# A transformer layer on one core: forget sums of the first FoX pair loaded earlier into another pool, late modulation begun earlier, and one ordering edge dropped in FoX

## The chip, the core and the metric

The kernel runs on one core of a Trainium2 chip. The metric is the time of one execution in microseconds (us). Before the change three runs took 3103.55 us in the median (3102.78 to 3106.61). TensorE (PE) multiplies matrices and transposes, and PEld is its weight load, shown apart. VectorE (DVE), ScalarE (ACT) and GpSimd (POOL) work elementwise. SyncE (SP) issues nearly all DMA transfers, one after the other in a fixed order: a transfer whose buffer is not free yet holds everything behind it in that queue.

## The reference

One decoder layer over 2048 tokens of width 1024, in float32:

```
mod = silu(c) @ w_ada + b_ada                  # six vectors: shift, scale, gate, twice
h = rms_norm(x, g_attn) * (1 + scale_a) + shift_a
q_f, k_f, v_f, q_s, k_s, v_s, f_logit = split(h @ w_in)
log_f = log_sigmoid(f_logit + b_fgate);  F = cumsum(log_f)
FoX, 8 heads:            softmax over s <= t of (q.k / 8 + F[t] - F[s]), times v
stick-breaking, 8 heads: A[t,s] = sigmoid(z_ts) * prod over s < j < t of (1 - sigmoid(z_tj)), times v
mix = concat(head_rms_norm(o_fox), head_rms_norm(o_sb))
x = x + gate_a * (mix @ w_out)
x = x + gate_m * (conv_ffn(rms_norm(x, g_mlp) * (1 + scale_m) + shift_m))
out = rms_norm(x, g_final)
```

F is the running sum of the log forget gates, one number per head and token; the text calls it the forget sums.

## The kernel before

Attention runs in 32 units: first 16 of stick-breaking, then 16 of FoX, each kind as four pairs of heads (p = 0 to 3) of four blocks of 512 tokens (tb = 0 to 3). A unit works through its two 256-query halves and its two heads. It forms logits on TensorE (lines 442 and 443, two matmuls of hi and lo parts), turns them into weights on DVE, ACT and POOL, transposes the weights on TensorE (L452), splits them into a high and a low part (ACT L456, DVE L457) and multiplies them with the values (L461). Later units of a pair have more keys and take longer.

Beside the attention run fillers. The projection of later units (`proj`, L284 for queries and keys, L355 for values) loads the modulated input `hs` in eight tiles of 512 KB (L410) into the ten buffers `hp`. `pace` says how many steps of it are due at each step of the attention, and `follow` draws them. From unit START = 3 on, the matmuls that a draw adds are tied behind the logits LAG = 12 entries back by `tc.issue_after`. That edge sets only an order on TensorE, no wait.

A second filler is the late modulation, `late_mod` (`lm`). It loads the convolution weights with 16 small DMAs (L593, L595) and transposes them. Then it goes through four of the six parts of `w_ada`: for each it loads eight 512 KB tiles (L607), scales them on ACT (L613) and sums them on POOL (L611, L614). Behind the first part comes `fold_out`: eight tiles of `w_out` are loaded (L577), scaled on DVE (L580), split on ACT and POOL and stored again (L584). All of this uses buffers of the same ten `hp`. It starts at unit LATE = 17, the second of FoX, with PER = 4 steps a unit.

In FoX a head needs its forget sums on all 128 partitions: tiles `Fb`, [128, 512], loaded from DRAM by a broadcasting DMA (L781), eight for each pair (two heads, four blocks). For the last chunk of keys POOL makes a masked copy `Fd` (L507). DVE adds `Fb` or `Fd` to the logits and keeps the row minimum `mn` (L509); ACT takes the exponential (L513).

Pools set the places. `px` holds the tiles of x for the first projection (tag `xt`, four buffers of [128, 1024]; later also the value tiles of stick-breaking pair 2) and small ones (tags `hf_a` and `z`). `sx` holds the intermediate tiles of stick-breaking. At the first FoX unit `sx` and `px` are closed and a pool `fx` is opened in their place, with ten buffers `Fb`, two `Fd`, one `sq` and others. A tile placed there has to wait for the last users of the old tiles at its place.

The order on each engine and in each queue comes from a scheduler that plays the program through when it is built: an instruction written later may be moved ahead of an earlier one that is not ready in that play.

Of the kernel before, what the change touches and what calls it, by code (L numbers as in the profile page):

```python
# [33 lines left out]
def kernel(ctx: ExitStack, tc: tile.TileContext, x, c, w_ada, b_ada, g_attn, w_in, b_fgate,  # L34
# [119 lines left out]
    def close_pool(*names):  # L154
        for name in names:
            pools.pop(name).close()
# [307 lines left out]
    def sb_head(j, qc, hl, Q, K, V, o):  # L464
        n = (2 * j + 2 + 3) // 4
        right = [None, None]
        for ch in range(n - 1, -1, -1):
# [18 lines left out]
            for m in range(0, nk, 2):  # L486
# [2 lines left out]
                         ch == n - 1 and m == 0, ch == 0 and m == nk - 2, kts[0] == 2 * j)  # L489
                yield  # L490

    def fox_head(j, qc, hl, Q, K, V, o, Fb, ls):
        n = (2 * j + 2 + 3) // 4
        rows_ = []
        for qi in range(2):
            W = (2 * j + qi + 1) * P
            a = sx.tile([P, S], F32, name="p", bufs=4)
            mn = None
            for ch in range(n):
                need = min(512, W - ch * 512)  # L500
                b = logits(max(need, 2 * P), slice((qc + qi) * P, (qc + qi + 1) * P), hl, Q, K[ch])
                sl = slice(ch * 512, ch * 512 + need)
                m2 = sx.tile([P, 1], F32, name="mn", bufs=8)
                add = Fb[ch]
                if ch == n - 1:
                    add = sx.tile([P, TB], F32, name="Fd", bufs=2)
                    nc.gpsimd.affine_select(out=add[:, :need], in_=Fb[ch][:, :need], pattern=[[-1, need]],  # L507
                                            base=need - P, channel_multiplier=1, compare_op=ALU.is_ge, fill=BIG)
                nc.vector.tensor_tensor_reduce(out=a[:, sl], in0=b[:, :need], in1=add[:, :need], scale=1.0,  # L509
                                               scalar=3e38 if mn is None else mn, op0=ALU.add, op1=ALU.min,  # L510
                                               accum_out=m2)
                mn = m2
            nc.scalar.activation(a[:, 0:W], a[:, 0:W], AF.Exp, scale=-1.0, bias=mn, accum_out=ls[:, hl, qc + qi:qc + qi + 1])  # L513
            rows_.append(a)
            yield
        for m in range(0, 2 * j + 2, 2):
            weighted(o, [m, m + 1], lambda kt, qi: rows_[qi][:, kt * P:(kt + 1) * P], V, hl, m == 0, m == 2 * j,
                     m == 2 * j)
            yield
# [10 lines left out]
    def attend(kind, p, tb, res, Fbs):  # L530
# [6 lines left out]
        mp = p if kind == "fox" else p + 4  # L537

        def head_var(j2):
            sq = sx.tile([P, 2 * P], F32, name="sq", bufs=1)  # L540
            cols_ = slice(j2 * 2 * P, (j2 + 1) * 2 * P)
            nc.gpsimd.tensor_mul(sq, oT[:, cols_], oT[:, cols_])

# [145 lines left out]
            yield max(first + (due - first) * min(1.0, m / (0.8 * n)),  # L689
                      base + (total - base) * (done + weight(units[i]) * m / n) / span if i >= START else 0)  # L690

    LAG = 12
    LATE, PER = 17, 4
    START, STOP = 3, 30

    HT = 2 * P
# [71 lines left out]
    for i, u in enumerate(units):  # L768
        kind, p, tb = u
        nxt = units[i + 1] if i + 1 < len(units) else None  # L770
        if u == ("sb", 1, 0):
            forget_sums()
        if u == ("fox", 0, 0):
            tick(1 << 20)
            close_pool("sx", "px")
            sx = open_pool("fx", side="right")
        if kind == "fox" and tb == 0:
            Fbs = [[sx.tile([P, TB], F32, name="Fb", bufs=10) for _ in range(NTB)] for _ in range(2)]
            for t in range(NTB):
                for h in range(2):  # L780
                    nc.sync.dma_start(Fbs[h][t],  # L781
                                      fs[2 * p + h:2 * p + h + 1, t * TB:(t + 1) * TB].to_broadcast([P, TB]))
        n = attend_steps(u)
        if i >= len(units) - 2:
            head_scale(i - len(units) + 2, pt(), sx)
# [9 lines left out]

        def follow(m):
            while projected[0] < goals[min(m, n - 1)]:
                with tc.issue_after(marks[max(0, len(marks) - 1 - LAG)]) if i >= START else nullcontext():
                    if next(ahead, 1) is not None:
                        break  # L800
            if nxt and projected[1] > i + 1 and loaded_units[0] == i + 1:
# [8 lines left out]
    tick(1 << 20)  # L810
    for t in range(2, NTB):
        head_scale(t, bank(psc, "bc", 2), p2a)
    close_pool("fx", "sb", "psb")

    psd = open_pool("psd", space=PSUM)
    ho = open_pool("hop0", side="right")
# [321 lines left out]
```

## Time and profile before

| | us |
|---|---|
| median of three runs | 3103.55 |
| the profiled execution, its own time | 3108.77 |
| its span, first to last instruction | 3106.8 |
| stick-breaking, to the store of its last unit | 0 to 884 |
| FoX, to about its last logits | 885 to 1540 |
| output projection | about 1540 to 1715 |
| up-projection and convolution | about 1715 to 2650 |
| down-projection | about 2650 to 3107 |

TensorE is busy for 95% of the span. Where the engine is busy all the time, the stage is as long as its matmuls. Idle stretches of TensorE, and stretches in which its granted clock (PEclk) is under 1, are what a change of order can win or lose. A row of the windows view gives, for a stretch of time, the length, then the busy time of PE, PEld, DVE, ACT and POOL with the number of instructions, then the granted clock, the busy share of the DMA engines and GB/s. In the timeline a row has start, length, engine, line and operation, and in brackets the idle time before it and what ended it.

### The profile page before, as it was taken

To read this page: it belongs to the slowest core of one execution; us is meant where nothing else is said; L and a number is where in the kernel's file an instruction comes from. 1 tells how busy PE (TensorE), PEld (TensorE's weight loads), DVE (VectorE), ACT (ScalarE), POOL (GpSimd) and SP (SyncE) were. 2 spreads that over 40 slices of the span, in tenths; PEclk is the share of its full clock that TensorE was granted. 3 is DMA by queue.
4 is the path that set the end of the run, shared out by engine and by line. 5 is a ranking of instruction groups with operands and counts; after the bars stand their busy time and mean duration, and the time that the engine had idled before them with its cause. 6 is when DMAs were issued, how large, how long until landed. Compare 5 with 4: busy or idle time off the path is not lost.

```text
span 3106.8 us, 45436 instructions
## 1 busy us (share of the span) xinstructions
PE 2957.1 (95%) x15934; PEld 2510.1 (81%) x15934; DVE 2063.9 (66%) x3206; ACT 1682.7 (54%) x3129; POOL 977.3 (31%) x1011
## 2 busy tenths in 40 slices
PE   6889999999989999999999899999999998999998
PEld 5788889889968888888877688888678887888887
DVE  6768778887856675667733677778977776254253
ACT  5657767777756665668634444444544443343332
POOL 1531322121122233333123344444444442332321
PEclk8999999999989999999999999999999999999999
DMA  9649756766387767775467522223222224565562
GB/s 270 228 133 318 217 186 204 265 222 215 123 265 235 223 217 271 241 266 162 167 197 228 189 76 82 83 87 89 85 82 82 82 82 145 184 203 166 183 203 86
DMA packets 312916, 546.79 MB, mean 176 GB/s; under 512 B 30992, under 2 KB 187408, under 8 KB 311664
## 3 DMA queue, kind: packets, MB, share of 16 engines
q1 hardware_dynamic: 301056, 531.27, 53.2%
q10 hardware_dynamic: 11632, 12.63, 1.2%
q8 instruction: 126, 2.06, 0.3%
q14 instruction: 102, 0.84, 0.1%
HBM read 407.14 MB, written 130.36 MB: 173 GB/s over the span
## 4 chain that ended last, share of the span: by engine, by line
PE 54%; DMA 15%; DVE 11%; POOL 7%; issue 7%; ACT 5%; SPq 1%; POOLq 0%; DVEq 0%; ACTq 0%
PE ps_pj L284 8%; PE ps_o L1077 8%; PE ps_pv L461 7%; PE ps_pt L452 6%; PE ps_pj L355 5%; PE ps_t L1077 4%; PE ps_bc L1077 4%; PE ps_qk L442 3%; PE ps_o L927 3%; PE ps_qk L443 3%; DMA wuraw<-in_w_up_dram 3%; DVE wu L45 3%; DMA hp<-in_w_ada_dram 2%; DVE u L996 2%; PE ps_o L736 2%
## 5 line engine op out<-in xcount | busy, mean ns | idle before, releaser
L927 PE MATMUL ps_o<-oa,wu 128*128 128x512 f32 x2088 | 505.6, 393 | 11.3 <-DVE oa L45 5.6
L927 PEld LDWEIGHTS ps_o<-oa,wu 128*128 128x128 f32 x2088 | 391.5, 189 | 103.2 <-DVE oa L45 9.3
L284 PE MATMUL ps_pj<-hp,w_qk 128*128 128x512 f32 x1512 | 417.0, 405 | 21.9 <-DMA hp<-hs 16.0
L457 DVE TENSOR_TENSOR at<-ps_pt,at 128x512 fp32r<-128x512 f32 (+1 forms) x576 | 364.9, 651 | 107.1 <-ACT at L456 104.5
L461 PE MATMUL ps_pv<-at,V 128*128 128x256 f32 x2304 | 408.2, 295 | 13.8 <-DVE at L457 5.6
L480 DVE TENSOR_TENSOR_SCAN a<-r,a 128x512 f32<-128x512 f32 (+2 forms) x320 | 363.1, 1153 | 82.8 <-POOL a L477 41.6
L456 ACT ACTIVATE at<-ps_pt 128x512 fp32r<-128x512 f32 (+1 forms) x576 | 319.3, 577 | 167.8 <-PE ps_pt L452 136.5
L461 PEld LDWEIGHTS ps_pv<-at,V 128*128 128x128 f32 x2304 | 336.7, 192 | 48.4 <-DVE at L457 14.6
L284 PEld LDWEIGHTS ps_pj<-hp,w_qk 128*128 128x128 f32 x1512 | 275.2, 191 | 79.0 <-DMA hp<-hs 20.8
L442 PE MATMUL ps_qk<-K,Q 128*128 128x512 f32 (+2 forms) x640 | 267.5, 419 | 20.4 <-DVE mn L509 11.7
L45 DVE TENSOR_TENSOR wd<-wdraw,wd 128x1024 fp32r<-128x1024 f32 x88 | 113.9, 1295 | 259.7 <-ACT wd L44 259.7
L1077 PE MATMUL ps_o<-wd,g 128*128 128x512 f32 x1040 | 250.1, 390 | 8.9 <-ACT g L44 8.9
L45 POOL TENSOR_TENSOR g<-graw,g 128x512 fp32r<-128x512 f32 x84 | 142.5, 1698 | 325.1 <-ACT g L44 317.9
L927 PE MATMUL ps_t<-ob,wu 128*128 128x512 f32 x984 | 241.8, 390 | 0.0
L443 PE MATMUL ps_qk<-K,Q 128*128 128x512 f32 (+2 forms) x640 | 238.7, 374 | 0.0
L1077 PEld LDWEIGHTS ps_o<-wd,g 128*128 128x128 f32 x1040 | 195.7, 188 | 50.0 <-ACT g L44 9.3
L355 PE MATMUL ps_pj<-w_v,hp 128*128 128x256 f32 (+1 forms) x1536 | 232.0, 289 | 3.6 <-DVE w_v L45 1.4
L44 ACT ACTIVATE wu<-wuraw 128x512 fp32r<-128x512 f32 x214 | 133.2, 626 | 188.4 <-PE ps_o L927 114.9
L355 PEld LDWEIGHTS ps_pj<-w_v,hp 128*128 128x128 f32 x1536 | 209.2, 191 | 13.6 <-DVE q L315 2.4
L927 PEld LDWEIGHTS ps_t<-ob,wu 128*128 128x128 f32 x984 | 185.3, 188 | 38.9 <-DVE y L979 0.2
L44 ACT ACTIVATE wd<-wdraw 128x1024 fp32r<-128x1024 f32 x88 | 93.0, 1057 | 207.0 <-PE ps_bc L1077 193.2
L474 ACT ACTIVATE r<-ps_qk 128x512 f32<-128x512 f32 (+2 forms) x320 | 172.9, 541 | 56.4 <-PE ps_qk L443 53.9
(222 smaller groups left out, 5490.1 us busy)
## 6 DMA issues: line engine op xcount, KB each, us to landing
hp<-hs SPq DMA_DIRECT2D x224, 512.0 KB
wuraw<-in_w_up_dram SPq DMA_DIRECT2D x84, 512.0 KB
wdraw<-in_w_down_dram SPq DMA_DIRECT2D x84, 512.0 KB
g<-u SPq DMA_DIRECT2D x42, 512.0 KB
graw<-g SPq DMA_DIRECT2D x84, 256.0 KB
hs<-hp SPq DMA_DIRECT2D x32, 512.0 KB
qk_fox<-q SPq DMA_DIRECT2D x32, 512.0 KB
Q<-qk_fox SPq DMA_DIRECT2D x64, 256.0 KB
```

The source lines that it names most:

```text
L44: nc.scalar.activation(hi, src, AF.Copy)
L45: (lo_engine or nc.gpsimd).tensor_sub(lo, src, f(hi))
L284: nc.tensor.matmul(acc, w[kt][:, a, n], h[:, bb], start=kt == 0 and i == 0, stop=kt == KT - 1 and i == 2)
L355: nc.tensor.matmul(av[:, t * width:(t + 1) * width], hts[kt][:, a, tok], w[1][kt][:, bb, 0:width], start=kt == 0 and m == 0, stop=kt == KT ...
L442: nc.tensor.matmul(b[:, :cw], Q[:, hl, 0, qcols], K[:, hl, :cw], start=True, stop=False)
L443: marks.append(nc.tensor.matmul(b[:, :cw], Q[:, hl, 1, qcols], K[:, hl, :cw], start=False, stop=True).ins)
L456: nc.scalar.activation(at[:, 0, lo:], b[:, lo:], AF.Copy)
L457: nc.vector.tensor_sub(at[:, 1, lo:], b[:, lo:], f(at[:, 0, lo:]))
L461: nc.tensor.matmul(o[:, 0:2 * P], V[kt // 4][:, kt % 4, hl, :], rhs, start=first and kk == 0 and w == 0, stop=last and kk == 1 and w == 1)
L480: nc.vector.tensor_tensor_scan(rev, r[:, 0:need][:, ::-1], rev, 0.0 if right[qi] is None else right[qi][:, 0:1], ALU.mult, ALU.add)
L927: nc.tensor.matmul(b, w[:, p, j], o[:, q], start=first and i == 0, stop=last and i == 2, skip_group_check=True)
L1077: nc.tensor.matmul(banks[t][n], g[:, a, t * P:(t + 1) * P], w[:, b, n * TB:(n + 1) * TB], start=k == 0 and i == 0, stop=k == NKD - 1 and i ...
```

## The change

There are four edits.

1. `Fb` becomes tiles of [128, 1024], each holding two blocks, in the four `xt` buffers of `px`, which now stays open through FoX: four loads of 512 KB a pair in place of eight of 256 KB. The first pair's loads are written at unit 14, two units ahead of FoX; those of the later pairs stay at the first unit of the pair. `Fd` and `sq` move into tags of `px` with two buffers each.
2. `late_mod` makes its first step (convolution weights) at unit 4 and the others from unit 12 on, the first unit of the last stick-breaking pair, three a unit in place of four.
3. `issue_after` is used for units 3 to 15 only, so not in FoX.
4. `px` is closed after FoX.

```diff
+    def load_sums(p):
+        sums = [[], []]
+        for t in range(0, NTB, 2):
+            for h in range(2):
+                b = px.tile([P, D], F32, name="Fb", tag="xt", bufs=4)
+                nc.sync.dma_start(b, fs[2 * p + h:2 * p + h + 1, t * TB:(t + 2) * TB].to_broadcast([P, D]))
+                sums[h] += [b[:, 0:TB], b[:, TB:D]]
+        return sums
...
-                    add = sx.tile([P, TB], F32, name="Fd", bufs=2)
+                    add = px.tile([P, TB], F32, name="Fd", tag="hf_a", bufs=2)
...
-            sq = sx.tile([P, 2 * P], F32, name="sq", bufs=1)
+            sq = (sx.tile([P, 2 * P], F32, name="sq", bufs=1) if kind == "sb" else
+                  px.tile([P, TB], F32, name="sq", tag="z", bufs=2)[:, 0:2 * P])
...
-    LAG = 12
-    LATE, PER = 17, 4
+    LAG, ENDQ = 12, 16
+    LATE, PER = 12, 3
...
         if u == ("sb", 1, 0):
             forget_sums()
+            next(lm)
         if u == ("fox", 0, 0):
             tick(1 << 20)
-            close_pool("sx", "px")
+            close_pool("sx")
             sx = open_pool("fx", side="right")
-        if kind == "fox" and tb == 0:
-            Fbs = [[sx.tile([P, TB], F32, name="Fb", bufs=10) for _ in range(NTB)] for _ in range(2)]
-            for t in range(NTB):
-                for h in range(2):
-                    nc.sync.dma_start(Fbs[h][t],
-                                      fs[2 * p + h:2 * p + h + 1, t * TB:(t + 1) * TB].to_broadcast([P, TB]))
+        if i == 14 or (kind == "fox" and tb == 0 and p):
+            Fbs = load_sums(p if kind == "fox" else 0)
...
-                with tc.issue_after(marks[max(0, len(marks) - 1 - LAG)]) if i >= START else nullcontext():
+                with tc.issue_after(marks[max(0, len(marks) - 1 - LAG)]) if START <= i < ENDQ else nullcontext():
...
-    close_pool("fx", "sb", "psb")
+    close_pool("fx", "px", "sb", "psb")
```

## The prediction, written before the changed kernel ran

> **What bounds the kernel now.** The page comes first: its span and the row of the granted clock, in 40 slices of 78 us.
>
> ```profile
> span 3106.8 us, 45436 instructions
> PEclk8999999999989999999999999999999999999999
> ```
>
> The slices say where to look, not why. The windows view over the stages that the change touches gives the lost time:
>
> ```profile
> 720.00:877.00 157.00, 155.93 (x1093) 143.92 (x1093) 126.24 (x170) 114.28 (x247) 19.85 (x36) 1.00 0.46 156
> 877.00:945.00 68.00, 54.98 (x274) 44.91 (x275) 30.49 (x88) 35.62 (x77) 24.16 (x33) 0.85 1.00 291
> 945.00:1540.00 595.00, 566.04 (x3710) 501.50 (x3709) 403.32 (x1033) 393.16 (x737) 180.29 (x243) 0.99 0.68 225
> 1540.00:1715.00 175.00, 158.53 (x746) 128.74 (x745) 65.56 (x120) 70.75 (x149) 47.45 (x57) 0.96 0.64 204
> ```
>
> In the last stick-breaking pair (720 to 877) TensorE idles 1.1 us of 157 at full clock: nothing is to be won there, only lost. At the passage into FoX (877 to 945) it idles 13.0 us of 68 and has a mean clock of 0.85, which is another 0.15 x 68 = 10.2 us: a hole of 23.2 us, with the DMA engines busy all the time (share 1.00). The rest of FoX idles 29.0 us of 595 and loses about 0.01 x 595 = 6 us of clock. I read the hole in steps of 4 us, then by its waits:
>
> ```profile
> 882.00:886.00 4.00, 1.14 (x6) 0.96 (x6) 0.16 (x1) 0.00 (x0) 0.00 (x0) 0.77 0.94 259
> 886.00:890.00 4.00, 2.69 (x7) 1.16 (x5) 0.00 (x0) 0.00 (x0) 0.00 (x0) 0.50 0.98 382
> 890.00:894.00 4.00, 4.00 (x12) 3.01 (x13) 1.27 (x7) 1.49 (x6) 1.45 (x5) 0.50 0.83 245
> ...
> 906.00:910.00 4.00, 1.76 (x4) 1.05 (x5) 2.38 (x7) 1.66 (x4) 2.84 (x5) 0.76 0.99 384
> 910.00:914.00 4.00, 4.00 (x28) 3.58 (x27) 3.53 (x12) 2.12 (x6) 0.99 (x3) 0.81 1.04 324
> 914.00:918.00 4.00, 2.33 (x13) 1.37 (x12) 3.03 (x11) 3.98 (x9) 4.00 (x5) 1.00 1.05 217
> 918.00:922.00 4.00, 3.67 (x12) 3.19 (x13) 0.65 (x3) 2.17 (x6) 2.34 (x3) 0.54 1.03 229
> 922.00:926.00 4.00, 4.00 (x21) 3.82 (x20) 1.23 (x4) 1.40 (x5) 0.00 (x0) 0.61 1.02 406
> ```
>
> The last column but two is the clock. It falls behind each hole in TensorE's work. Four microseconds at 0.50 cost 2.0 us, so the three losses are: 882 to 894, 0.92 + 2.0 + 2.0 = 4.9 us; 906 to 914, 0.96 + 0.76 = 1.7 us; 918 to 926, 1.84 + 1.56 = 3.4 us. Together that is 10.0 of the 10.2 us.
>
> The chain of work that ended last (start, length, what) goes through transfers here, so these microseconds count in full:
>
> ```profile
> 876.25 7.63 DMA V<-vs_fox
> ...
> 886.80 8.20 DMA Fb<-fs
> ...
> 906.68 11.60 DMA hp<-hs
> ```
>
> One of the three is of the sums; values and `hs` hold the others. The waits of TensorE in 877 to 945:
>
> ```profile
> PE ps_pj L284 <- DMA hp<-hs: 6.1, 4, 2.9
> PE ps_qk L442 <- DVE mn L509: 4.8, 1, 4.8
> ```
>
> And in 945 to 1540:
>
> ```profile
> PE ps_pj L284 <- DMA hp<-hs: 8.8, 8, 2.4
> PE ps_qk L442 <- DVE mn L509: 6.9, 10, 2.3
> PE ps_pv L461 <- ACT at L456: 4.6, 5, 2.0
> PE ps_pt L452 <- DVE at L457: 2.8, 1, 2.8
> ```
>
> The timeline shows what stands behind them:
>
> ```profile
> 877.48 0.60 PE L452 MATMUL ps_pt<-edge,a 128*128 128x128 f32 x4
> 877.84 1.32 PE L461 MATMUL ps_pv<-at,V 128*128 128x256 f32 x8
> 885.30 7.17 SPq L781 DMA_DIRECT2D Fb<-fs  x8
> 891.83 0.64 POOL L507 TENSOR_SCALAR_AFFINE_SELECT Fd<-Fb 128x128 f32<-128x128 f32 x2 [10.08 <-DMA Fb<-fs]
> 904.02 3.11 POOL L611 TENSOR_SCALAR hp<-hp,cs 128x512 f32<-128x512 f32 x2 [8.62 <-DMA hp<-in_w_ada_dram]
> 908.24 0.79 PE L442 MATMUL ps_qk<-K,Q 128*128 128x512 f32 x1 [4.76 <-DVE mn L509]
> ...
> 1086.53 1.41 DVE L580 SCALAR_TENSOR_TENSOR hp<-hp,cols 128x512 f32<-128x512 f32 x2 [3.38 <-DMA hp<-in_w_out_dram]
> 1088.60 0.81 PE L452 MATMUL ps_pt<-edge,p 128*128 128x128 f32 x4 [2.80 <-DVE at L457]
> 1102.63 0.69 PE L442 MATMUL ps_qk<-K,Q 128*128 128x384 f32 x1 [2.29 <-DVE mn L509]
> ```
>
> The sums are issued at 885.30, behind the last stick-breaking work, and POOL can mask only at 891.83. At 904.02 POOL has waited 8.62 us for a tile of the late modulation, with the next masks queued behind it; DVE, and then the logits at 908.24, wait for them. At 1086.53 the same happens on DVE: the fold of `w_out` waits 3.38 us for its DMA at the head of DVE's queue, and TensorE idles 2.80 us for a split that stands behind it.
>
> **The change, part by part.** The sum is made on the profiled execution, 3108.77 us (span 3106.8 and 2.0 around it); that is 5.2 us above the median of the runs, 3103.55, and I carry the difference over unchanged.
>
> *The passage.* In the order of the changed kernel the four loads stand behind the values of stick-breaking pair 2, some 300 us early, and the first masks are made before the passage. The late modulation's first tiles are summed before it too, so no L611 stands in front of a mask. The 4.8 us wait goes whole: -4.8. What is late next are the `hs` tiles. Half of them still stand in SP's queue behind the store of the last stick-breaking unit, but the eight sums (7.17 us of issue) and the 16 convolution DMAs no longer stand around them: I take half of the 6.1 us, -3.0. The thin end of the stick-breaking chain stays. Of the clock, the 1.7 us behind the wait that goes returns whole, and a third of the other two losses, (4.9 + 3.4) / 3 = 2.8: -4.5. Not more, because two of the chain's three transfers stay; but in the changed order the keys of the last block stand in SP's queue ahead of that store, no longer behind the sums. Together -12.3, between 0 (the transfers keep the hole open) and -23.2.
>
> By the Trainium skill's page "TensorE: Matmul & The Clock Gate" (Part 1: The HAM clock gate) the clock halves only after about one idle window of 3.4 us and returns after as long a busy one, so holes shorter than that would cost no clock. The half clock at 886 to 894 agrees with the lower of its two rates. By it the whole 10.2 us would return, in place of 4.5, and the sum would be lower by 5.7. The row 918 to 922 speaks against it: 0.54 behind a window with 1.67 us idle.
>
> *The fold of `w_out`* moves from about 1010 to 1190 into about 880 to 1010. It leaves the start of the second pair, where it and its clock cost this:
>
> ```profile
> 1088.00:1092.00 4.00, 3.40 (x15) 3.01 (x16) 4.00 (x12) 3.35 (x8) 2.97 (x3) 0.62 0.43 167
> 1092.00:1096.00 4.00, 4.00 (x19) 3.60 (x18) 3.94 (x11) 2.85 (x7) 1.25 (x2) 0.53 1.00 306
> ...
> 1100.00:1104.00 4.00, 1.71 (x9) 1.22 (x9) 3.51 (x8) 3.72 (x8) 1.96 (x3) 0.83 1.05 410
> 1104.00:1108.00 4.00, 4.00 (x26) 3.81 (x26) 3.69 (x10) 2.79 (x5) 1.76 (x3) 0.74 0.96 334
> ```
>
> That is 2.8 + 2.3 us of waits and 4 x (0.38 + 0.47 + 0.17 + 0.26) = 5.1 us of clock, 10.2 in all. But its loads now meet the stretch where the DMA engines have no share left, and a late one stands again at the head of DVE's queue, in front of L509. Bounds are -10.2 (nothing comes back) and +10.2 (twice as much does). I take +2: the same again and a little more, since the share is 1.00 there.
>
> *The rest of the late modulation in stick-breaking.* Until FoX there are 14 scalings on ACT, at this row:
>
> ```profile
> L613 ACT ACTIVATE hp<-hp,cs x56: 706/712/735, 913.1 to 1430.9; 128x512 f32<-128x512 f32 x56
> ```
>
> 14 x 0.712 = 10.0 us on an ACT that is busy 114.28 of 157 us there, POOL 19.85, DMA share 0.46: covered by TensorE's own work, 0. If ACT were the bound it would be the 10.0. The 16 small DMAs now stand in SP's queue in unit 4, behind the forget sums; their transposes stand far behind on TensorE: 0.
>
> *A new wait in SP's queue.* The third load of the sums reuses the value tile of pair 2, which waits for the DMA and the subtraction of these rows:
>
> ```profile
> L399 SPq DMA_DIRECT2D xt<-vd x4: 370/370/377, 404.3 to 557.1; - x4
> L400 POOL TENSOR_TENSOR xt<-xt x4: 2389/2390/2681, 408.3 to 561.4; 128x1024 f32<-128x1024 f32 x4
> ```
>
> The last pair of these is issued at 557.1 and done at 561.4 + 2.4 = 563.8: SP stands 6.3 us there (less its own 0.4), with the queries of a later unit and six `hs` tiles behind it. Those are drawn ahead of use, so +1, between 0 and +6.3.
>
> *No queueing in FoX.* Projections may now fill any gap of TensorE in the played order. Beyond the passage the waits that filling could cover are 6.9 + 4.6 + 2.8 = 14.3 us, and 6 us of clock hang on them; but matmuls drawn earlier meet `hs` loads that are less far ahead, and TensorE takes them in order: the 8.8 us could double. I take a third of 14.3 as won (-4.8) and a fifth of 8.8 as lost (+1.8), -3. Bounds: -20.3 and +8.8.
>
> *Four sum buffers in place of ten.* Before, two of ten were spare, and the second pair's loads began some 50 us before its start:
>
> ```profile
> 1023.04 0.33 SPq L781 DMA_DIRECT2D Fb<-fs  x1
> ```
>
> Now head 1's first tile is free only after its last use by the last head of the pair before. Behind that head's logits come eight groups of four transposes and four value matmuls, 8 x (0.60 + 1.32 / 2) = 10.1 us of TensorE. A load took 891.83 - 885.30 = 6.5 us from issue to use. It is covered with 3.6 us to spare: +1 for the three starts, between 0 and +29.7 (6.5 us and 3.4 us of clock at each).
>
> Sum: -12.3 + 2 + 0 + 1 - 3 + 1 = -11.3. 3108.77 becomes 3097.5; in the median of runs 3103.55 - 11.3 = 3092.2, so **3092 us**.
>
> **The rivals.** *The hole only moves.* The fold's loads fill the saturated stretch and its DVE step stands in front of the first FoX heads (+10.2 in place of +2), and the early matmuls win nothing (0 in place of -3): -11.3 + 8.2 + 3 = -0.1, 3103.5 us. For it speaks the share 1.00 from 877 to 945 and the chain's transfers; against it that 2 MB of sums and the first `w_ada` tiles leave that stretch.
>
> *Slower: the pair starts wait for sums.* If SP reaches the load of head 1's first tile late, each of three starts loses 9.9 us: -11.3 - 1 + 29.7 = +17.4, 3121 us. It decides from (12.3 + 6.2) / 3 = 6.2 us a start. For it: these loads now wait at the head of SP's queue with keys and queries behind them. Against it: the 3.6 us to spare, and head 0's tiles come free a whole head earlier.
>
> *The filling does more.* All 14.3 us of waits and their 6 us of clock go, -20.3 in place of -3: 3103.55 - 11.3 - 17.3 = 3075 us. Against it: most of these waits are chains through DVE that already have projections around them.
>
> *Short holes cost no clock* (the full 10.2 us comes back): 3103.55 - 11.3 - 5.7 = 3086.5 us. This is what the page's rule gives.
>
> **How the numbers follow.** Two tenths of a percent, 6.2 us, is about what can be told from no change. The forecast has 0.42, the hole that moves 0.21, the slow pair starts 0.22, the filling 0.10, short holes without cost 0.05. Faster: 0.42 + 0.10 + 0.05 = 0.57; same 0.21; slower 0.22. The range runs from 3075 (half of the filling case below it) to 3112 (some two thirds of the slow case above it). The forecast's own range is 3083 to 3097.
>
> **What would show it.** Right: no TensorE wait on `mn` near the passage, the 68 us around it with at most 7 us idle and a clock above 0.92, sums landed before 600 us. The fold right: DVE waits for `w_out` between 880 and 1010 of 3 us or so, none near 1086. Wrong: idle TensorE at the start of pairs 1 to 3 with POOL or DVE waiting for `Fb`; TensorE waits on `hs` well over 11 us in the rest of FoX; idle time in the last stick-breaking pair above 3 us.

## The result and the profile after

The changed kernel takes 3087.88 us in the median of four runs (3084.52 to 3089.98), against 3104.79 us for the kernel before beside it (3102.78 to 3106.61). The ratio of the new time to the old is 0.9945, with a 95% interval of 0.9927 to 0.9962: faster by 16.9 us. The forecast was 3092 us; its range of 3075 to 3112 holds the measured time, and so does the forecast's own range of 3083 to 3097. The sum was 5.6 us short of the gain, and the experiments below show that its terms were further off than their sum.

From the page of the profiled execution after (its own time is 3089.98 us):

```profile
span 3088.3 us, 45418 instructions
PEclk8999999999999999999999999999999999999999
```

The slices say as little as before. In the windows view of the kernel after (columns as in the prediction), the stages are:

```profile
600.00:720.00 120.00, 114.07 (x723) 99.48 (x722) 96.55 (x118) 91.96 (x203) 47.09 (x52) 1.00 0.72 236
720.00:877.00 157.00, 154.03 (x1055) 140.71 (x1054) 127.28 (x172) 115.29 (x249) 27.39 (x42) 0.99 0.49 162
877.00:945.00 68.00, 61.72 (x383) 54.13 (x383) 50.42 (x119) 45.53 (x99) 22.83 (x29) 0.95 0.95 306
945.00:1520.00 575.00, 555.84 (x3667) 495.71 (x3666) 391.49 (x1008) 380.25 (x714) 162.46 (x228) 0.99 0.67 224
```

Two rows of the kernel before for the same bounds, which the prediction did not show:

```profile
600.00:720.00 120.00, 117.42 (x758) 103.75 (x756) 96.96 (x127) 91.29 (x206) 28.27 (x42) 1.00 0.70 223
945.00:1520.00 575.00, 546.74 (x3586) 484.94 (x3585) 386.48 (x994) 379.10 (x717) 177.13 (x238) 0.99 0.70 231
```

Three things happened. At the passage (877 to 945) TensorE is busy for 61.72 us in place of 54.98, at a clock of 0.95 in place of 0.85. In the rest of FoX (945 to 1520) it is busy 9.1 us longer within the same 575 us. And in stick-breaking it has become worse: from 600 to 720 it idles 5.9 us in place of 2.6, from 720 to 877 3.0 us in place of 1.1. So the last unit of stick-breaking ends later (its store is issued at 894.64 us in place of 883.95), and FoX is shorter by more than the whole gain: 652.1 us from that store to the last of FoX (1546.76), in place of 680.7 (883.95 to 1564.65). The late end is not projection done early: up to that store TensorE has made 940 projection matmuls of L284 into `ps_pj`, where it had made 948 in the kernel before (L355: 1152 in both). From 600 us to the store it idles 12.2 us in place of 7.2, and the half clock of the hole shown next now falls before the store.

The passage in steps of 4 us, after:

```profile
882.00:886.00 4.00, 2.89 (x25) 2.69 (x24) 2.07 (x3) 2.26 (x6) 0.57 (x1) 1.00 1.01 301
886.00:890.00 4.00, 1.79 (x8) 1.32 (x9) 4.00 (x5) 1.59 (x4) 3.75 (x2) 0.66 1.07 276
890.00:894.00 4.00, 4.00 (x19) 3.85 (x19) 1.87 (x4) 2.04 (x6) 0.00 (x0) 0.50 1.01 330
894.00:898.00 4.00, 3.45 (x19) 2.69 (x18) 1.85 (x10) 2.94 (x9) 1.73 (x4) 0.99 1.03 414
...
902.00:906.00 4.00, 2.95 (x21) 2.39 (x20) 4.00 (x10) 3.88 (x10) 1.40 (x3) 1.00 1.04 319
906.00:910.00 4.00, 2.72 (x19) 2.13 (x18) 3.94 (x11) 2.40 (x6) 3.08 (x5) 1.00 1.01 240
```

Of the three holes one is left, at the thin end of the stick-breaking chain (882 to 894); it is made of two waits, 1.80 and 1.52 us. Behind it the row of 902 to 910 shows 2.3 us idle with no loss of clock. TensorE's waits, after, first for 867 to 945 and then for 945 to 1530 (total, times, longest):

```profile
PE ps_pt L452 <- DVE a L480: 3.3, 2, 1.8
PE ps_qk L442 <- DVE mn L518: 1.7, 2, 1.2
...
PE ps_pj L284 <- DMA hp<-hs: 7.6, 3, 4.8
...
PE ps_pv L461 <- ACT at L456: 3.5, 5, 0.8
```

Near the passage no wait on `hs` is left, and the 4.8 us one on `mn` is down to 1.7 in two. Further on the waits on `mn` are gone from the head of the list. The timeline after shows the sums and the one new wait, and below it stands what SP waited for at the sums between 1200 and 1240:

```profile
555.94 6.44 SPq L497 DMA_DIRECT2D Fb<-fs  x3
570.80 0.32 SPq L497 DMA_DIRECT2D Fb<-fs  x1
...
1219.74 0.53 SPq L497 DMA_DIRECT2D Fb<-fs  x1
1220.87 0.52 SPq L497 DMA_DIRECT2D Fb<-fs  x1
1228.07 0.33 SPq L410 DMA_DIRECT2D hp<-hs  x1
1235.07 2.63 PE L284 MATMUL ps_pj<-hp,w_qk 128*128 128x512 f32 x6 [4.75 <-DMA hp<-hs]
```
```profile
SPq L497 <- DVE mn L518: 16.4, 2, 15.2
```

The first pair's sums are issued some 310 us ahead of FoX. Before the third pair SP stands 15.2 us (to 1208.30) at a load of sums whose buffer VectorE still reads, and then 5.5 us at a load of keys. The last two sums go out at 1219.74 and 1220.87, and the `hs` tile behind them, with loads of queries and keys between, at 1228.07: TensorE stands 4.75 us for it. How much of that the sums alone cost is not shown.

For the comparisons below I use one measure, lost TensorE time: in windows of 4 us, the idle time plus (1 - granted clock) x 4, summed over a stage. It counts an idle microsecond at a low clock a little twice, as the prediction's 23.2 us did. The passage is the 68 us from 14 us before the store of the last stick-breaking unit to 54 us behind it; the rest of FoX goes from there to its last logits. The runs were made in three series, in which the kernel before measured 3104.6, 3106.9 and 3107.6 us. So each ratio is against the kernel before of its own series, and effects in microseconds are the ratio's distance from 1 times 3104 us.

### The profile page after: what moved, and what is told of

The parts are those of the page before. It is cut to its first block, busy times and chain, and to the rows that moved or that the text cites. A ratio compares the mean times of both kernels' runs of the same rounds, so it can differ in the third digit from the quotient of the medians.

```text
span 3088.3 us, 45418 instructions
## 1 busy us (share of the span) xinstructions
PE 2951.0 (96%) x15934; PEld 2510.9 (81%) x15934; DVE 2075.5 (67%) x3206; ACT 1682.6 (54%) x3129; POOL 992.2 (32%) x1011
## 4 chain that ended last, share of the span: by engine, by line
PE 57%; DMA 12%; DVE 12%; POOL 7%; issue 7%; ACT 4%; SPq 1%; POOLq 0%; ACTq 0%; DVEq 0%
PE ps_pj L284 8%; PE ps_o L1084 8%; PE ps_pv L461 7%; PE ps_pt L452 6%; PE ps_pj L355 5%; PE ps_t L1084 4%; PE ps_bc L1084 4%; PE ps_qk L442 3%; PE ps_o L746 3%; PE ps_o L934 3%; PE ps_qk L443 3%; DMA wuraw<-in_w_up_dram 3%; DVE wu L45 3%; DVE u L1003 2%; POOL wuraw L921 2%
## 5 line engine op out<-in xcount | busy, mean ns | idle before, releaser
L284 PE MATMUL ps_pj<-hp,w_qk 128*128 128x512 f32 x1512 | 421.1, 406 | 13.3 <-DMA hp<-hs 7.6
L480 DVE TENSOR_TENSOR_SCAN a<-r,a 128x512 f32<-128x512 f32 (+2 forms) x320 | 374.0, 1186 | 86.3 <-POOL a L477 45.1
L461 PE MATMUL ps_pv<-at,V 128*128 128x256 f32 x2304 | 406.3, 293 | 17.4 <-DVE at L457 6.3
L284 PEld LDWEIGHTS ps_pj<-hp,w_qk 128*128 128x128 f32 x1512 | 274.5, 191 | 65.4 <-DMA hp<-hs 8.7
L442 PE MATMUL ps_qk<-K,Q 128*128 128x512 f32 (+2 forms) x640 | 264.7, 414 | 11.4 <-ACT a L475 6.0
L355 PE MATMUL ps_pj<-w_v,hp 128*128 128x256 f32 (+1 forms) x1536 | 237.1, 290 | 2.6 <-DVE w_v L45 1.3
L355 PEld LDWEIGHTS ps_pj<-w_v,hp 128*128 128x128 f32 x1536 | 211.8, 192 | 12.4 <-DVE q L315 2.1
L44 ACT ACTIVATE wd<-wdraw 128x1024 fp32r<-128x1024 f32 x88 | 93.1, 1058 | 206.2 <-PE ps_bc L1084 190.9
```

What stands on the lines that cost most here:

```text
L44: nc.scalar.activation(hi, src, AF.Copy)
L284: nc.tensor.matmul(acc, w[kt][:, a, n], h[:, bb], start=kt == 0 and i == 0, stop=kt == KT - 1 and i == 2)
L355: nc.tensor.matmul(av[:, t * width:(t + 1) * width], hts[kt][:, a, tok], w[1][kt][:, bb, 0:width], start=kt == 0 and m == 0, stop=kt == KT ...
L442: nc.tensor.matmul(b[:, :cw], Q[:, hl, 0, qcols], K[:, hl, :cw], start=True, stop=False)
L461: nc.tensor.matmul(o[:, 0:2 * P], V[kt // 4][:, kt % 4, hl, :], rhs, start=first and kk == 0 and w == 0, stop=last and kk == 1 and w == 1)
L480: nc.vector.tensor_tensor_scan(rev, r[:, 0:need][:, ::-1], rev, 0.0 if right[qi] is None else right[qi][:, 0:1], ALU.mult, ALU.add)
```

## The experiments

I call the edits S (forget sums in the pool of x, first pair early; edit 1 with 4), L (late modulation from unit 12; edit 2) and Q (no queueing in FoX; edit 3). L with Q, without S, was not run, and no run parts the early loading in S from its change of buffers.

| kernel | ratio, 95% interval | us | lost, 600 us to passage | passage | rest of FoX |
|---|---|---|---|---|---|
| before | 1 | 0 | 2.9 | 24.0 | 35.8 |
| S | 0.9982 (0.9972 to 0.9992) | -5.6 | 4.1 | 13.2 | 33.5 |
| L | 1.0017 (1.0005 to 1.0029) | +5.3 | 11.3 | 28.7 | 29.7 |
| Q | 0.9946 (0.9932 to 0.9960) | -16.8 | 8.5 | 17.4 | 26.4 |
| S + L | 0.9958 (0.9940 to 0.9975) | -13.0 | 8.1 | 10.8 | 31.6 |
| S + Q | 0.9937 (0.9923 to 0.9951) | -19.6 | 4.1 | 9.0 | 27.4 |
| S + L + Q, the change | 0.9945 (0.9927 to 0.9962) | -17.1 | 10.6 | 9.7 | 22.6 |

### The forget sums alone

The kernel before with edits 1 and 4, that is, with the change's `LATE`, `next(lm)` and tie taken back:

```diff
-    LAG, ENDQ = 12, 16
-    LATE, PER = 12, 3
+    LAG, ENDQ = 12, 32
+    LATE, PER = 17, 4
...
-            next(lm)
```

> The kernel before with the first edit alone: forget sums in the pool of x, the first pair's loaded two units ahead; late modulation and the tied projections as before. Theory (the sums make the hole at the passage into FoX): the hole of 23 us in 877 to 945 shrinks to about 12, the logits no longer wait for a mask, and the time is 9 to 14 us under the kernel before, 3091 to 3096 us. Rival (the hole is made by the transfers that fill the DMA engines there, and by the late modulation's first tiles): the hole stays above 18 us and the time is within 5 us of before.

Measured: 3099.34 us, 5.6 us faster by the ratio, which is less than the theory expected and about at the edge of its rival. The hole closes as its term said (24.0 to 13.2 lost, 10.8 less; the term was 12.3). In the windows view of this kernel the passage is:

```profile
877.00:945.00 68.00, 58.24 (x342) 49.47 (x342) 39.52 (x102) 43.30 (x92) 25.56 (x33) 0.95 0.96 303
```

From trace to trace this agrees with the time: 10.8 us less in the passage, 2.3 less in the rest of FoX, 1.2 more between 600 us and the passage and 2.6 more before (7.5 to 10.1 from 200 to 600) are 9.3 us, and the profiled executions' own times differ by 9.5 (3108.77 and 3099.24). The runs give 5.6 (2.5 to 8.7), because the profiled execution of before lies 5 us above the median of its runs. The rest of FoX still loses 33.5 us. One place there shows how. The timeline of this kernel, DVE and then TensorE, and the same stretch in the windows view:

```profile
1161.50 1.41 DVE L590 SCALAR_TENSOR_TENSOR hp<-hp,cols 128x512 f32<-128x512 f32 x2 [4.14 <-DMA hp<-in_w_out_dram]
...
1163.97 0.79 PE L442 MATMUL ps_qk<-K,Q 128*128 128x512 f32 x1 [5.12 <-DVE mn L518]
```
```profile
1160.00:1164.00 4.00, 0.03 (x1) 0.04 (x1) 2.50 (x6) 1.64 (x4) 0.95 (x1) 0.70 0.93 310
1164.00:1168.00 4.00, 4.00 (x17) 3.81 (x18) 3.32 (x10) 3.13 (x6) 1.85 (x3) 0.50 0.95 288
1168.00:1172.00 4.00, 4.00 (x25) 3.50 (x24) 2.11 (x6) 1.50 (x3) 0.00 (x0) 0.95 1.04 402
```

DVE stands 4.14 us at the fold of `w_out`, at the head of its queue, for a transfer. The row minimum behind it is late, the logits that need its buffer wait, and TensorE, which takes its matmuls in order, idles 5.12 us and then runs at half clock. It is the mechanism that the prediction read at 1086.53 in the kernel before.

### No early late modulation (S + Q)

```diff
-    LATE, PER = 12, 3
+    LATE, PER = 17, 4
...
-            next(lm)
```

> The changed kernel with the second edit undone: late modulation from the second FoX unit on, four steps a unit, its first step there too. Theory (the early sums of w_ada cost the stick-breaking units what they stand in front of on POOL and ACT): the unit in which they begin, pair 2's last, takes about 72 us again in place of 82.9, stick-breaking ends near 884, and of the gain of 16.9 us some part is lost again in FoX; if the early sums are a net loss the time is under 3088 by up to 7 us. Rival (the early late modulation is what empties FoX of traffic): the stick-breaking end comes 10 us earlier but FoX takes 20 us longer, and the time is 3094 to 3100 us.

Measured: 3085.13 us, not separated from the whole change (0.9937 against 0.9945). Against S alone, Q takes another 14.0 us; by the measure 4.2 of it lie in the passage and 6.1 in the rest of FoX, and the remainder is not located. The timeline of this kernel shows what Q does at the fold's next tile, DVE first, then TensorE:

```profile
1156.52 1.42 DVE L590 SCALAR_TENSOR_TENSOR hp<-hp,cols 128x512 f32<-128x512 f32 x2 [3.94 <-DMA hp<-in_w_out_dram]
...
1152.92 1.63 PE L284 MATMUL ps_pj<-hp,w_qk 128*128 128x512 f32 x6
1156.81 1.87 PE L284 MATMUL ps_pj<-hp,w_qk 128*128 128x512 f32 x7
```
```profile
1152.00:1156.00 4.00, 4.00 (x25) 3.48 (x24) 0.58 (x3) 1.09 (x2) 0.00 (x0) 1.00 1.05 314
1156.00:1160.00 4.00, 4.00 (x23) 2.87 (x22) 3.48 (x7) 1.61 (x3) 1.28 (x1) 1.00 1.03 284
```

DVE waits nearly as long (3.94 us), but TensorE has projection matmuls in its order at this spot (L284 is 4.7 us of its work from 1152 to 1160), and stays busy at full clock. In S alone it has none at all from 1148 to 1168. The waits of the two kernels between 945 and 1530 say the same in sum, S alone first, then S + Q:

```profile
PE ps_qk L442 <- DVE mn L518: 10.9, 7, 5.1
DVE hp L590 <- DMA hp<-in_w_out_dram: 8.5, 4, 4.1
```
```profile
PE ps_qk L442 <- DVE mn L518: 4.5, 8, 1.3
DVE hp L590 <- DMA hp<-in_w_out_dram: 11.3, 5, 3.9
```

VectorE waits longer for `w_out` with Q than without, and TensorE less for `mn`. At these places Q does not remove the waits of VectorE; it lays work under them. Other waits do shrink with it: ScalarE stands 13.2 us for `w_ada` in S + Q and 30.2 in S alone (945 to 1530); what of Q's gain that makes is not parted.

### The queue kept (S + L)

```diff
-    LAG, ENDQ = 12, 16
+    LAG, ENDQ = 12, 32
```

> The changed kernel with the third edit undone: the projections stay tied 12 logits back in FoX too. Theory (untied projections fill the gaps in the rest of FoX): TensorE's idle time from 945 to the last logits rises from 19 us to about 29, and the time is 6 to 10 us over the changed kernel, 3094 to 3098 us. Rival (the ties cost nothing, the gain is of the other two edits): within 3 us of the changed kernel, 3085 to 3091 us.

Measured: 3095.51 us, 13.0 us faster than before. With S in place, L is worth 7.4 us (-13.0 against -5.6), though it puts 4.0 us more of lost time into stick-breaking (4.1 to 8.1): it takes 2.4 out of the passage and 1.9 out of the rest of FoX. The fold is part of that: DVE waits once for `w_out` in this kernel, 2.0 us. By these stages the two kernels differ by only 0.3 us, and the profiled execution was among the longer of its kernel (3097.07 us, its runs 3089.30 to 3100.76). So the sign of the 7.4 us is measured (the two intervals give it about 6 us either way), and its place is not.

One hole stands out in this trace, ScalarE's wait first and then TensorE's:

```profile
1064.52 1.33 ACT L623 ACTIVATE hp<-hp,cs 128x512 f32<-128x512 f32 x2 [8.51 <-DMA hp<-in_w_ada_dram]
...
1066.53 1.95 PE L461 MATMUL ps_pv<-at,V 128*128 128x256 f32 x5 [8.04 <-ACT at L456]
```

ScalarE stands for a tile of `w_ada` at the head of its queue, the split behind it is late, and TensorE has nothing to lay under it: with the clock behind it that is 13.3 us lost from 1058 to 1074. In the changed kernel TensorE waits at most 0.8 us for that split.

### No queueing alone (Q)

```diff
-                with tc.issue_after(marks[max(0, len(marks) - 1 - LAG)]) if i >= START else nullcontext():
+                with tc.issue_after(marks[max(0, len(marks) - 1 - LAG)]) if START <= i < 16 else nullcontext():
```

> The kernel before with the third edit alone: projections not tied in FoX. Theory (untied projections fill gaps): 4 to 10 us under before, 3095 to 3101 us, with the hole at the passage still about 20 us, since the masks there wait for the sums. Rival (untied projections only draw hs loads earlier and wait for them): within 3 us of before or above it.

Measured: 3088.21 us, 16.8 us faster and well below the 3095 to 3101 us expected: one line alone gives what the whole change gives. Its profiled execution was its longest (3096.59 us), so its trace understates it; even so 6.6 us of lost time leave the passage and 9.4 the rest of FoX, while 5.6 come up between 600 us and the passage. The prediction feared that matmuls drawn earlier would meet `hs` tiles that are less far ahead. The waits of this kernel, 945 to 1530, say no:

```profile
PE ps_qk L442 <- DVE mn L509: 6.3, 9, 1.8
PE ps_pj L284 <- DMA hp<-hs: 4.3, 3, 3.1
```

The waits on `hs` are halved (8.8 us before), not doubled.

### Early late modulation alone (L)

```diff
-    LATE, PER = 17, 4
+    LATE, PER = 12, 3
...
+            next(lm)
```

> The kernel before with the second edit alone: the late modulation starts in the last stick-breaking pair, three steps a unit; the forget sums and the ordering edge in FoX stay as before. Theory (the edit moves w_ada's transfers and sums into units 10 to 12, where they cost some 4 to 7 us of TensorE's time, and frees FoX of as much or a little more; the kept-edge run without it and with it differ by 3.8 us in its favour): 3098 to 3103 us, lost TensorE time in stick-breaking from 600 us on of 8 us or more where before has 2.9, and a passage that stays open at 20 us or more. Rival (the edit is worth its few us only where the passage is closed, so that there is room behind it): 3105 us or more.

Measured: 3113.27 us, slower by 5.3 us. The rival is right: L is worth its microseconds only where the sums have left the passage. In the windows view and TensorE's waits (870 to 950) of this kernel:

```profile
600.00:720.00 120.00, 114.38 (x723) 99.81 (x722) 94.01 (x122) 91.44 (x203) 48.32 (x53) 1.00 0.72 232
...
877.00:945.00 68.00, 49.01 (x253) 39.97 (x254) 34.18 (x84) 34.01 (x77) 15.63 (x25) 0.82 0.95 323
```
```profile
PE ps_pj L284 <- DMA hp<-hs: 15.1, 4, 6.6
```

TensorE idles 5.6 us between 600 and 720, about as in the changed kernel, and the passage is worse: TensorE now stands 15.1 us for `hs` there. The chain that ended last goes there through a store of the fold (8.42 us from 897.88), the sums (8.31 from 906.32) and a load of the fold (7.63 from 914.65). So the fold's transfers meet the sums, which is the first half of the prediction's rival "the hole only moves".

### The late modulation's sums on VectorE

To find what L costs stick-breaking, the changed kernel with the scaling and sums of the first part of `w_ada` moved from GpSimd to VectorE:

```diff
-                        nc.gpsimd.tensor_scalar_mul(wsum[:, sl], w[:, sl], cs[:, 0:1])
+                        (nc.vector if part == 2 else nc.gpsimd).tensor_scalar_mul(wsum[:, sl], w[:, sl], cs[:, 0:1])
...
-                        nc.gpsimd.tensor_add(wsum[:, sl], wsum[:, sl], w[:, sl])
+                        (nc.vector if part == 2 else nc.gpsimd).tensor_add(wsum[:, sl], wsum[:, sl], w[:, sl])
```

> The changed kernel with the scaling and the sums of the first part of the late modulation (the one that now runs in stick-breaking) on VectorE in place of GpSimd. Theory (GpSimd's sums, 18.2 us of its waits between 629 and 724 us, stand ahead of the stick-breaking masks for which VectorE waits at L480): the lost TensorE time between 600 us and the passage falls from 10.6 us to about 4, and the time to 3081 to 3084 us. Rival (the loss comes from ScalarE, which stands at the scaling of a tile of w_ada that has not landed, L623, 7.5 us of waits; that stays): the lost time stays at 9 to 12 us and the time at 3087 to 3090 us, or above where VectorE's own work is delayed.

The waits of the changed kernel between 629 and 724 us on which the two theories rested:

```profile
POOL hp L624 <- ACT hp L623: 18.2, 5, 7.4
ACT hp L623 <- DMA hp<-in_w_ada_dram: 7.5, 5, 3.5
```

Measured: 3083.40 us, ratio 0.9919 (0.9899 to 0.9939), which overlaps the whole change's interval. The windows view of this kernel, to be held against the same rows above:

```profile
600.00:720.00 120.00, 114.10 (x729) 100.16 (x729) 100.27 (x132) 92.94 (x205) 26.68 (x39) 1.00 0.75 238
...
945.00:1520.00 575.00, 560.47 (x3704) 499.99 (x3705) 393.96 (x1018) 384.01 (x720) 161.52 (x226) 0.99 0.65 222
```

GpSimd is relieved (26.68 us in place of 47.09), and TensorE idles exactly as long from 600 to 720 (5.90 in place of 5.93 us). From 600 us to the passage it loses 16.9 us by the measure, in place of 10.6. So my theory fell: taking the sums off GpSimd won nothing there. VectorE, which has them now (100.27 us busy in place of 96.55), may have lost what GpSimd won; the run does not part the two. The 3081 to 3084 us that the theory named came out, but for another reason: what is gained stands in the passage (4.6 us lost in place of 9.7) and in FoX (560.47 us busy in place of 555.84). The waits of ScalarE for `w_ada` remain as a suspect (5.2 us here), but no run took them away alone.

### How far back the tie is

S + Q, but with a tie in FoX at 24 entries, and in another kernel at 18, in place of none:

```diff
-                with tc.issue_after(marks[max(0, len(marks) - 1 - LAG)]) if START <= i < ENDQ else nullcontext():
+                with tc.issue_after(marks[max(0, len(marks) - 1 - (LAG if i < ENDQ else 2 * LAG))]) if i >= START else nullcontext():
```

> The run without the early late modulation (3085.13 us), but in FoX the projection's matmuls are again tied behind logits, 24 entries back instead of 12. Theory (the edge costs by how late it lets the projection fill gaps): between the run with the edge at 12 (3099.3 us) and the one without (3085.1 us), at 3088 to 3096 us. Rival (it is the mere presence of an order, whatever its distance, because the edge places the projection in a fixed spot in TensorE's queue): within 2 us of 3099 us. Other rival (12 entries are just short of what is needed): within 2 us of 3085 us.

> The run without the early late modulation, the projection in FoX tied 18 entries back (12 back gave 3099.3 us, 24 back 3083.4 us, no edge 3085.1 us). Theory (the cost is how late the edge lets the projection come, so it falls with distance): between the two, 3086 to 3094 us. Rival (there is a threshold, and beyond some distance the edge is never what holds the projection back): within 2 us of 3083.4 us, or within 2 us of 3099.3 us.

Measured: 0.9923 (0.9903 to 0.9943) at 24 and 0.9972 (0.9961 to 0.9983) at 18, beside 0.9982 at 12 and 0.9937 without a tie. In microseconds: -5.6 at 12, -8.7 at 18, -23.9 at 24, -19.6 with none. At 24 the tie costs nothing that can be measured; at 18 most of its cost is still there, and 18 is not told from 12. The rest of FoX loses 33.5, 35.0, 23.3 and 27.4 us in the same order. So the cost goes between 18 and 24 in the main, nearer to a threshold than to the even fall that I expected. The 3083.41 us at 24 are where that run's last rival put them; the 3096.41 us at 18 lie outside both my range and its rival's.

### The tie in stick-breaking

S + Q without any tie, and S + Q with 24 entries in both kinds:

```diff
-                with tc.issue_after(marks[max(0, len(marks) - 1 - LAG)]) if START <= i < ENDQ else nullcontext():
+                with tc.issue_after(marks[max(0, len(marks) - 1 - LAG)]) if False else nullcontext():
```
```diff
-    LAG, ENDQ = 12, 16
+    LAG, ENDQ = 24, 16
...
-                with tc.issue_after(marks[max(0, len(marks) - 1 - LAG)]) if START <= i < ENDQ else nullcontext():
+                with tc.issue_after(marks[max(0, len(marks) - 1 - LAG)]) if i >= START else nullcontext():
```

> The run without the early late modulation (3085.13 us), with the ordering edge dropped in stick-breaking too (units 3 to 15). Theory (the edge costs wherever it stands, by delaying filling work): stick-breaking has only 10.9 us of lost TensorE time between 200 and 600 us and 4.1 us from there on, so at most a few us can be won: 3079 to 3085 us. Rival (in stick-breaking the projection drawn early takes the work away that the later units, the longest, need for filling): 3088 us or more, with over 10 us lost between 600 us and the passage.

> The run with the edge 24 entries back in FoX (3083.4 us), with 24 in stick-breaking too in place of 12. Dropping the edge there altogether cost 12.3 us (3097.4 against 3085.1 us), with 19.7 us lost between 200 and 600 us in place of 10.9. Theory (in stick-breaking the projection drawn early pushes the logits back, the more the further it may come ahead): 3086 to 3094 us. Rival (24 entries hold it enough there as well): within 2 us of 3083.4 us.

Measured: 3097.41 us, 0.9963 (0.9951 to 0.9976), without any tie, 8 us worse than S + Q and in the rival's range. With 24 everywhere 3104.89 us, 0.9998 (0.9987 to 1.0009), 23 us worse than with 24 in FoX alone, and worse than theory and rival named. So in stick-breaking the tie at 12 is needed; of what was tried there, nothing else comes near it. The windows view from 200 to 600, first with 12 there (24 in FoX), then without any tie, then with 24 everywhere:

```profile
200.00:600.00 400.00, 392.51 (x2565) 348.95 (x2564) 314.35 (x416) 282.92 (x617) 97.00 (x134) 1.00 0.72 237
```
```profile
200.00:600.00 400.00, 383.69 (x2477) 339.97 (x2476) 298.69 (x395) 268.65 (x588) 97.03 (x130) 0.99 0.71 235
```
```profile
200.00:600.00 400.00, 387.39 (x2507) 344.56 (x2507) 300.12 (x400) 272.06 (x597) 93.54 (x131) 0.99 0.72 239
```

TensorE idles 16.3 and 12.6 us in place of 7.5, and VectorE and ScalarE, which carry the stick-breaking chain, have done less in the same time. The store of the last stick-breaking unit is issued at 949.61 and 920.79 in place of 889.53. The projection that came ahead took the place of logits on which that chain waits: by 400 us TensorE has made 456 and 454 projection matmuls of L284 in place of 426, and 105 and 108 logits of L442 in place of 114. By the measure, 24 everywhere is worse than no tie in the later stages (15.2 us lost against 9.0 from 600 us to the passage, 24.5 against 20.1 in the rest of FoX); why is not shown.

### Two combinations

The changed kernel with VectorE's sums and 24 in FoX, and the same with the late modulation from unit 15 (`LATE, PER = 15, 4`):

```diff
-                        nc.gpsimd.tensor_add(wsum[:, sl], wsum[:, sl], w[:, sl])
+                        (nc.vector if part == 2 else nc.gpsimd).tensor_add(wsum[:, sl], wsum[:, sl], w[:, sl])
...
-                with tc.issue_after(marks[max(0, len(marks) - 1 - LAG)]) if START <= i < ENDQ else nullcontext():
+                with tc.issue_after(marks[max(0, len(marks) - 1 - (LAG if i < ENDQ else 2 * LAG))]) if i >= START else nullcontext():
```

> The changed kernel with the first part's sums on VectorE (3083.4 us) and with an edge 24 entries back in FoX in place of none. Theory (an edge at 24 back keeps the filling for the later units of a pair without holding it up; without the early late modulation it read 1.7 us below no edge, which its interval doesn't separate): 3079 to 3084 us. Rival (the early late modulation leaves nothing for such an order to keep): 3083 to 3087 us.

> As the run with VectorE's sums and the edge at 24, but the late modulation goes on at unit 15 with four steps a unit, so that only its first steps fall into stick-breaking. Theory (the transfers and sums of w_ada cost stick-breaking some 7 to 13 us of TensorE's time, 10.6 and 16.9 us lost there against 4.1 without them; started at its last unit they cost less and still fill the passage): lost time from 600 us to the passage under 8 us and 3076 to 3082 us. Rival (what is kept in stick-breaking comes back as waits in FoX, where the same transfers then fall): 3083 to 3088 us.

Measured: 3090.60 us, 0.9953 (0.9936 to 0.9970), and 3090.51 us, 0.9947 (0.9929 to 0.9966): slower than both theories and both rivals named. Neither adds to the parts. The first is 10.6 us slower by the ratio than VectorE's sums without a tie, a little more than the 8 us that the intervals leave open. In the second, stick-breaking is healed as expected (3.9 us lost from 600 us to the passage), and the rest of FoX loses 35.0 us in place of 24.2 in the first, as its rival feared. So the lowest medians are those of the tie at 24 (3083.41) and of VectorE's sums (3083.40). No interval sets either clearly apart from S + Q or from the change.

## Why the prediction was right, and where its terms were wrong

The sign and the range were right, and the total is partly luck. Put by edit, the forecast was -10.3 for S (the passage, which counts on L too, and the two waits of the sums), +2 for L and -3 for Q. In that order the runs give S -5.6, then L -7.4, then Q -4.1: S gave 4.7 us less than forecast, L 9.4 more and Q 1.1 more. What failed is that the terms were added. L measures +5.3 us alone, -7.4 behind S, and +2.5 behind S and Q. Q measures -16.8 alone, -14.0 behind S, and -4.1 behind S and L. The intervals set L behind S clearly apart from L alone (12.7 us, give or take 7), and Q behind S just apart from Q behind S and L (9.9, give or take 9). S and Q do add up within theirs (-19.6 against -22.4). The three edits alone, -5.6, +5.3 and -16.8, add up to the same -17.1 by chance.

*The passage, -12.3.* In its own place this was right. "No TensorE wait on `mn` near the passage" held but for 1.7 us, "at most 7 us idle" came out at 6.3 and "clock above 0.92" at 0.95, and the sums landed before 600 us. With S alone the passage lost 10.8 us less. Three things were wrong. The hole was read from an execution 5.2 us longer than the median, and that difference was carried over unchanged; against the runs S is worth 5.6 us (2.5 to 8.7), not 12.3. The passage was not S's alone: Q by itself took 6.6 us out of it, with all sums still there. And the chain of three transfers left out a fourth that it has in the hole, keys, 10.21 us from 895.82. Of the clock, I took 4.5 of 10.2 us as coming back. In 877 to 945 the loss is 0.05 x 68 = 3.4 us after, so about 6.8 came back.

*The fold, +2.* The move was harmless: VectorE waited once for `w_out`, 2.1 us, where it waited 5.6 in three before. The wait that was read at 1086.53 shows again in S alone, and what was feared of the full DMA engines shows in L alone. Outside the passage +2 was written for L (with 0 for its stick-breaking part), and it measures +5.3 without S and -7.4 behind it, of which the traces put 2.4 in the passage: the sign was wrong for L behind S, the order of the sum.

*The rest of the late modulation in stick-breaking, 0.* Wrong: by the measure L adds 8.4 us from 600 us to the passage alone, 4.0 behind S and 6.5 behind S and Q. The bound of 10.0 held. I reasoned from TensorE being busy from 720 to 877, but the schedule moved the work further ahead, into 600 to 720, where 3.3 us of idle time appeared. The sign named for it, idle time in the last pair above 3 us, came out at 3.0 for that pair; the larger part stood one pair earlier, where I had not looked.

*The wait of the third sums load, +1, and four buffers, +1.* The first three loads went out between 555.94 and 562.38, with two waits of SP of 2.5 us each, close to the 6.3 us that were read, and TensorE did not wait for `hs` from 550 to 620. The fourth went out at 570.80. No pair start had VectorE or GpSimd wait for `Fb`, so the rival "slower: pair starts wait for sums" fell. A cost came by what is queued behind: SP stood 15.2 us at the sums, and ahead of one of three pair starts an `hs` tile came 4.75 us late. The sums' share in that is not shown.

*No queueing in FoX, -3.* This is the term that was furthest off as a statement about the kernel before. It measures -16.8 alone and -14.0 behind S. Behind S and L it measures -4.1, which the intervals don't tell from 0 nor from -11, and the trace has 9.0 us less lost in the rest of FoX (31.6 to 22.6), a difference that the one hole at 1066.53 in S + L (13.3 us) more than makes up. The mechanism was there, "projections may now fill any gap", and its bound of -20.3 holds every one of these. The size was wrong because I let a third of the waits be covered and added a cost for `hs` that came out as a gain (8.8 to 4.3 us in Q alone, 7.6 in the change), and because I counted only the waits beyond the passage, while Q fills there too. So the rival "the filling does more" describes Q in the kernel before better than the forecast's own split. Its 3075 us was too much for the change, where Q behind S and L is worth -4.1 and not -20.3; what L and Q take from each other is not explained beyond that.

*Short holes cost no clock.* Not borne out as a rule for this kernel: with one hole left, of 1.80 and 1.52 us of waits in 882 to 890, the clock fell to 0.66 and then 0.50. By the Trainium skill's page "TensorE: Matmul & The Clock Gate" (Part 1: The HAM clock gate) about one idle window of 3.4 us halves the clock. The trace agrees in the rows 902 to 910, where 2.3 us idle in pieces of at most 1.2 cost no clock, and in S alone, where 5.12 us in one piece cost 4 x (0.30 + 0.50 + 0.05) = 3.4 us of it. It does not agree in 882 to 894.

## What to carry to other kernels

An ordering edge between filling work and the main chain has a price in each stage by itself: here a tie 12 entries back was needed in stick-breaking and cost 14 to 17 us in FoX as long as all of the late modulation ran there, and 18 back was still too close where 24 cost nothing. Where waits of a few microseconds stay in the main chain, ask first what TensorE has in its order beneath them, before moving transfers to make them shorter. Edits that move the same transfers have to be measured together and apart: one of them was a loss alone and a gain behind the other.

## What the runs showed of the hardware

A hole costs its clock unevenly. A wait of 5.12 us in S alone took 3.4 us of clock with it. The 4.75 us wait at 1235.07 in the changed kernel took less, by its windows:

```profile
1230.00:1234.00 4.00, 0.31 (x3) 0.11 (x1) 1.44 (x3) 0.60 (x1) 0.00 (x0) 1.00 0.87 316
1234.00:1238.00 4.00, 2.94 (x9) 2.41 (x10) 0.69 (x1) 1.16 (x2) 0.00 (x0) 0.68 0.82 265
1238.00:1242.00 4.00, 4.00 (x33) 4.00 (x33) 2.07 (x7) 4.00 (x13) 3.75 (x5) 0.89 0.63 192
```

That is 4 x (0.32 + 0.11) = 1.7 us, half as much for nearly the same hole. Short waits can cost as much as long ones. First the kernel before, then two waits of the changed kernel:

```profile
918.33 1.65 PE L284 MATMUL ps_pj<-hp,w_qk 128*128 128x512 f32 x3 [1.98 <-DMA hp<-hs]
...
886.69 0.41 PE L452 MATMUL ps_pt<-edge,a 128*128 128x128 f32 x2 [1.80 <-DVE a L480]
888.74 0.69 PE L452 MATMUL ps_pt<-edge,a 128*128 128x128 f32 x2 [1.52 <-DVE a L480]
```

Behind the 1.98 us the kernel before lost 3.4 us of clock (918 to 926), and behind its wait of 4.76 us ahead of 908.24 only 1.7. The 1.80 and 1.52 us, half a microsecond of work apart, cost 4 x (0.34 + 0.50 + 0.01) = 3.4 us (886 to 898), while 1.05 and 1.18 us in 902 to 910 cost none. So a hole's length alone does not give its price. What does, these rows do not show.
